# Branch A of a hybrid encoder layer: values, both tiles' transposes in three banks, then scores, in one step

## The chip, the cores and the metric

The kernel runs on one core of one Trainium2 chip. The metric is the device time of one execution in microseconds (us), the median of the runs; lower is better.

## The reference, cut to what matters

One encoder layer is computed for two inputs, a prompt of 256 rows and a sample of 1024 rows, each row 1024 wide, in float32. The layer has two attention branches beside each other, gates that merge them, an output projection, and an MLP with a squared ReLU. The change lies in branch A, a windowed attention with a sink: eight query heads over two key/value heads, 64 wide, each block of 128 rows looking at its own block of keys and the two next to it.

```python
s = jnp.einsum('bnqgrd,bnkgd->bngrqk', qb, kb).astype(jnp.float32) * (dh ** -0.5)
logits = jnp.where(valid[None, :, None, None], s + bias, NEG_INF)
m = jnp.maximum(jnp.max(logits, axis=-1), sink_r)
p = jnp.exp(logits - m[..., None])
denom = jnp.sum(p, axis=-1) + jnp.exp(sink_r - m)
o = jnp.einsum('bngrqk,bnkgd->bnqgrd', p.astype(vb.dtype), vb).astype(jnp.float32)
o = o / jnp.transpose(denom, (0, 1, 4, 2, 3))[..., None]
...
gates = jax.nn.sigmoid((z[..., o6:] + b_gate).astype(jnp.float32)).astype(x.dtype)
merged = gates[:, :, 0] * (o_a.reshape(b, S, A_Q) @ w_branch_a) + gates[:, :, 1] * (o_b @ w_branch_b)
x = x + merged @ w_out
```

## The kernel before, in words

The large products are split into a high and a low part and take three matmuls each; they fill most of the time. Branch A comes about a third of the way in, after the projections and branch B. From there on the instructions of each engine stand in the order in which the Python code writes them; there is no planner.

Branch A works on 40 tiles: four units (`u`, two query heads each) times ten tiles (`t`) of 128 query rows, eight of the sample and two of the prompt. A tile looks at two or three key blocks of 128, so it is 256 or 384 wide: tiles 0, 7, 8 and 9 of a unit are 256 wide, the others 384. For each tile there are four pieces of work:

- `scores` (lines 1116 to 1132): per head two matmuls on TensorE (PE) into a bank tagged `sc`, a custom VectorE (DVE) instruction that adds the bias and takes the row maximum (L1126), and one small DVE instruction for both heads that makes the negative maximum `nm_a` (L1130).
- `exponential` (L1136): per head one ScalarE (ACT) instruction in place on `s`, with the row sum.
- `transposes` (L1139): per head and key block one PE transposition of 128 x 128 (L1148), four or six in all, into two banks tagged `pt`. ACT empties the first bank (four transpositions, L274), DVE the second (two, L276; none for a tile 256 wide). They go to a buffer `pt` of six blocks, of which there are two.
- `values_of` (L1152): for a pair of tiles, the products of the transposed exponentials with the values (L1163) into the one bank tagged `pv`, a DVE copy to `o` (L1166) and a store that GpSimd (POOL) issues (L1167).

PSUM has eight banks: three tagged `mm`, two `sc`, two `pt`, one `pv`.

Between these pieces the loop (lines 1384 to 1419) draws portions of other work from two generators. `fill` is `logits`, the last five blocks of 128 columns of the gate logits: each `next(fill)` issues four matmuls 512 wide or eight 256 wide into an `mm` bank (L192). A block of 512 columns takes six portions, one of 256 columns three; each set of 128 gate columns has the blocks 512, 256, 512. Where a block is complete, the next call first writes ACT's copy to `gs` (L1188) and its store, and after the 256 block also the conversion of the next weights: `whi` on ACT (L231) and `wlo` on DVE (L235). `merges` is `merge`, which combines branch B's three groups: its later portions load `r` by SyncE's queue (L1284, L1287) and multiply and add on POOL (L1303, L1306).

The loop handles a pair of tiles per step, 20 steps and one more to empty the pipeline. A step at `j` computes scores for tiles `j` and `j + 1`, transposes tiles `j - 2` and `j - 1`, and multiplies out tiles `j - 4` and `j - 3`. Its order on PE is: scores of `j`, fill, values, fill, transposes of `j - 2`, scores of `j + 1`, fill, transposes of `j - 1`.

Of the kernel before, what the change touches and what calls it, by code (L numbers as in the profile page):

```python
# [97 lines left out]
def encoder_kernel(  # L98
# [37 lines left out]
    def bank(tag, name=None):  # L136
        return psum.tile([P, 512], F32, name=name or tag, tag=tag, bufs={"mm": 3, "sc": 2, "pt": 2, "pv": 1}[tag])
# [133 lines left out]
    def moved(eng, out, in_):  # L271

        if eng is nc.scalar:
            nc.scalar.activation(out, in_, AF.Copy)  # L274
        else:
            nc.vector.tensor_copy(out, in_)  # L276
# [825 lines left out]
    if True:  # L1102
# [3 lines left out]
        def a3(name, shape=(P, 2, 3 * P), n=3, dt=F32):  # L1106
            return att.tile(list(shape), dt, name=name, tag=name, bufs=n)
# [8 lines left out]
        def scores(u, t):  # L1116
            st, bias = units[u]
            lo, W, c0 = tiles[t]
            s = a3("s", n=3)
            m = small.tile([P, 2], F32, name="m", tag="m")  # L1120
            for h in range(2):
                ps = bank("sc")
                q = st["q"][h][:, P * t : P * t + P]
                nc.tensor.matmul(ps[:, :W], q, st["k"][1][:, P * lo : P * lo + W], start=True, stop=False)  # L1124
                nc.tensor.matmul(ps[:, :W], q, st["k"][0][:, P * lo : P * lo + W], start=False, stop=True)
                nc.vector.tensor_tensor_reduce(  # L1126
                    s[:, h, :W], ps[:, :W], bias[:, h, c0 : c0 + W], 1.0, -3.0e38,
                    op0=ALU.add, op1=ALU.max, accum_out=m[:, h : h + 1],
                )
            nc.vector.scalar_tensor_tensor(nm_a[:, 2 * u : 2 * u + 2, t], m, -1.0, nsink[:, 2 * u : 2 * u + 2],  # L1130
                                           op0=ALU.mult, op1=ALU.min)
            live[u, t] = s
# [5 lines left out]

        def transposes(u, t):  # L1139

            W = tiles[t][1]
            s = live[u, t]
            pt = a3("pt", (P, 6, P), 2)
            jobs = [(b, h) for b in range(W // P) for h in range(2)]
            for i, eng in ((0, nc.scalar), (4, nc.vector))[: 1 + (len(jobs) > 4)]:
                ps, e = bank("pt"), min(len(jobs), i + 4)
                for k, (b, h) in enumerate(jobs[i:e]):
                    nc.tensor.transpose(ps[:, P * k : P * k + P], s[:, h, P * b : P * b + P], ident)  # L1148
                moved(eng, pt[:, i:e, :], ps[:, : P * (e - i)].rearrange("p (i q) -> p i q", q=P))
            live[u, t] = pt  # L1150

        def values_of(u, t):  # L1152

            pv = bank("pv")
            for i in range(2):
                lo, W, _ = tiles[t + i]
                pt = live.pop((u, t + i))
                v, rest = units[u][0]["v"]
                for b in range(W // P):
                    k = lo + b  # L1160
                    src = v[:, k, HALVES[u // 2]] if k < 8 else rest[:, k - 8, HALVES[u // 2]]
                    for h in range(2):
                        nc.tensor.matmul(pv[HALVES[h], P * i : P * i + P], src, pt[:, 2 * b + h, :],  # L1163
                                         start=b == 0, stop=b == W // P - 1, skip_group_check=True)
# [159 lines left out]
    if True:  # L1324
# [57 lines left out]
        next(merges)  # L1382
        steps_of(fill, 2)
        for j in range(0, n + 2, 2):
            if j < n:
                scores(*order[j])
                next(fill)
                for h in range(2):
                    exponential(*order[j], h)
            if j > 2:  # L1390
                values_of(*order[j - 4])
                if j < n:
                    next(merges, None)
            next(fill)
            if j:
                transposes(*order[j - 2])
            if j == n:
                next(fill)
            if j < n:
                scores(*order[j + 1])  # L1400
                next(fill)
            if j:
                transposes(*order[j - 1])
                if j > 2:
                    next(merges, None)
            if j < n:
                for h in range(2):
                    exponential(*order[j + 1], h)
            if j == n - 4:
                high_b(0)  # L1410
                low_b(0)
            if j < n and order[j][1] == 0 and order[j][0] < 3:
                u = order[j][0] + 1
                units[u] = load_unit(u), load_bias(u, lambda name, shape: a3(name, shape, 2))
            if j in (n - 6, n - 4):
                fetch()
            if j == n - 2:
                load_o(0)
                load_o(1)
# [574 lines left out]
```

## Time and profile before

| | us |
|---|---|
| median of 3 runs | 1694.82 |
| lowest and highest | 1693.9 and 1695.1 |
| the profiled execution | 1694.27 |
| its span in the profile | 1692.5 |
| PE busy, share of the span | 1675.2, 99% |
| DVE busy | 953.4, 56% |
| ACT busy | 719.6, 43% |
| POOL busy | 513.1, 30% |
| branch A's loop, from the span's start | about 547 to 684 |

In the profile, a row of the timeline has the start and the duration in us, the engine, the source line, the operation, what it writes and reads, and a count where equal neighbours are merged; brackets hold the idle time of the engine ahead of it and what ended that. PEld is the load of a matmul's weights, which runs beside the matmul ahead of it. Matmuls overlap: the duration of one is longer than the distance to the next start, so distances between starts are what counts on PE.

### The profile page before, as it was taken

What the parts mean: (1) busy time and instruction counts of PE and PEld (TensorE: products, weight loads), DVE (VectorE), ACT (ScalarE), POOL (GpSimd) and SP (SyncE); (2) the same over time, 40 slices, a digit from 0 to 9 for tenths busy, and PEclk for the clock granted to TensorE, in tenths of its full rate; (3) what the DMA queues carried; (4) which work ended last, traced back from release to release, by engine and by line L of the source; (5) the groups of instructions that cost most, each with busy time, mean ns of one, the idle gap of its engine ahead of it and who ended that gap; (6) DMA issues with size and microseconds to landing.
All of it is one profiled execution on the core that took longest, in us unless ns stands there. A gap on an engine that the chain in (4) does not pass through costs nothing.

```text
span 1692.5 us, 24900 instructions
## 1 busy us (share of the span) xinstructions
PE 1675.2 (99%) x9268; PEld 1415.3 (84%) x9268; DVE 953.4 (56%) x1548; ACT 719.6 (43%) x1489; POOL 513.1 (30%) x404
## 2 busy tenths in 40 slices
PE   8999999999999999999999999999999999999998
PEld 7898888887778888888888888888888888888886
DVE  6732233445553565577278444545547867667575
ACT  6332323345563655654175333333334333333345
POOL 1312212212111463200100555546456332314150
PEclk9999999999999999999999999999999999999999
DMA  7426562566666793845121443443346845633333
GB/s 245 150 58 126 133 137 75 162 192 189 186 191 182 218 244 107 282 141 206 38 85 61 160 141 114 142 158 116 123 159 231 299 152 159 210 104 116 119 118 125
DMA packets 224409, 260.36 MB, mean 154 GB/s; under 512 B 29568, under 2 KB 154288, under 8 KB 224288
## 3 DMA queue, kind: packets, MB, share of 16 engines
q1 hardware_dynamic: 214976, 235.60, 44.1%
q0 software_dynamic: 7936, 20.54, 5.7%
q10 hardware_dynamic: 1376, 2.62, 0.4%
q8 instruction: 73, 1.20, 0.3%
q14 instruction: 48, 0.39, 0.1%
HBM read 173.03 MB, written 90.92 MB: 156 GB/s over the span
## 4 chain that ended last, share of the span: by engine, by line
PE 92%; DVE 3%; ACT 2%; DMA 1%; issue 1%; POOL 0%; SPq 0%; DVEq 0%; ACTq 0%
PE dn L349 20%; PE x L349 19%; PE mm L192 14%; PE z L349 9%; PE v L788 6%; PE mm L349 5%; PE y L349 5%; PE sc L349 3%; PE pv L349 3%; PE sc L538 1%; PE pv L1163 1%; PE pv L581 1%; PE pt L568 1%; PE pt L1148 1%; PE sc L1124 1%
## 5 line engine op out<-in xcount | busy, mean ns | idle before, releaser
L349 PE MATMUL dn<-dhi,ulo 128*128 128x512 f32 x448 | 174.6, 390 | 3.1 <-DVE ulo L186 3.1
L349 PE MATMUL dn<-dhi,uhi 128*128 128x512 f32 x448 | 174.3, 389 | 0.0
L349 PE MATMUL dn<-dlo,uhi 128*128 128x512 f32 x448 | 174.3, 389 | 0.0
L349 PE MATMUL x<-chi,wlo 128*128 128x512 f32 x424 | 167.4, 395 | 1.7 <-DVE wlo L316 1.6
L349 PE MATMUL x<-clo,whi 128*128 128x512 f32 x424 | 165.8, 391 | 0.1
L349 PE MATMUL x<-chi,whi 128*128 128x512 f32 x424 | 165.1, 389 | 0.0
L316 DVE TENSOR_TENSOR wlo<-ta,whi 128x1024 fp32r<-128x1024 f32 x30 | 55.8, 1859 | 180.4 <-ACT whi L314 180.4
L316 DVE TENSOR_TENSOR wlo<-raw,whi 128x1024 fp32r<-128x1024 f32 x60 | 91.3, 1522 | 101.1 <-ACT whi L314 101.1
L391 POOL TENSOR_TENSOR tb<-raw 128x512 f32<-128x512 f32 x25 | 32.6, 1304 | 364.5 <-DMA raw<-in_w_in_dram 145.2
L349 PEld LDWEIGHTS dn<-dhi,ulo 128*128 128x128 f32 x448 | 84.1, 188 | 21.6 <-DVE ulo L186 4.3
L186 DVE TENSOR_TENSOR ulo<-uraw,uhi 128x1024 fp32r<-128x1024 f32 x56 | 95.1, 1719 | 11.6 <-ACT uhi L185 11.6
L349 PEld LDWEIGHTS dn<-dhi,uhi 128*128 128x128 f32 x448 | 84.1, 188 | 17.5
L349 PEld LDWEIGHTS dn<-dlo,uhi 128*128 128x128 f32 x448 | 84.1, 188 | 17.4
L349 PEld LDWEIGHTS x<-chi,wlo 128*128 128x128 f32 x424 | 79.8, 188 | 20.0 <-issue 1.7
L349 PEld LDWEIGHTS x<-chi,whi 128*128 128x128 f32 x424 | 79.6, 188 | 17.0
L349 PEld LDWEIGHTS x<-clo,whi 128*128 128x128 f32 x424 | 79.8, 188 | 14.9 <-DVE clo L316 0.4
L1692 POOL TENSOR_TENSOR t<-raw,t 128x1024 f32<-128x1024 f32 x16 | 46.3, 2909 | 142.6 <-DMA raw<-in_w_down_dram 138.1
L1846 DVE TENSOR_TENSOR v<-v,dn 128x512 f32<-128x512 f32 x90 | 59.5, 681 | 39.8 <-PE dn L349 35.2
L558 ACT ACTIVATE s<-s,nm_b 128x128 f32<-128x128 f32 (+1 forms) x120 | 51.9, 434 | 54.4 <-DVE nm_b L550 54.4
L349 PE MATMUL dn<-dhi,up 128*128 128x512 f32 x224 | 73.5, 389 | 0.0
L1939 POOL TENSOR_TENSOR u<-u,u 128x640 f32<-128x640 f32 x16 | 25.6, 1597 | 156.5 <-ACT u L1864 156.5
L349 PE MATMUL z<-chi,wlo 128*128 128x512 f32 x184 | 72.1, 392 | 0.0
(325 smaller groups left out, 4651.4 us busy)
## 6 DMA issues: line engine op xcount, KB each, us to landing
scr_u<-u SPq DMA_DIRECT2D x112, 320.0 KB, 2.6
uraw<-scr_u SPq DMA_DIRECT2D x56, 512.0 KB, 4.5
raw<-in_w_in_dram SPq DMA_DIRECT2D x33, 512.0 KB, 5.9
raw<-in_w_up_dram SPq DMA_DIRECT2D x32, 512.0 KB, 5.3
raw<-in_w_down_dram SPq DMA_DIRECT2D x28, 512.0 KB, 6.6
sg<-scr_g SPq DMA_DIRECT2D x32, 256.0 KB, 6.2
uraw<-scr_u SPq DMA_DIRECT2D x28, 256.0 KB, 4.6
v<-scr_v SPq DMA_DIRECT2D x96, 64.0 KB, 2.8
```

Of the source, the lines that this page charges most:

```text
L186: nc.vector.tensor_tensor(lo, src, hi.bitcast(F32), op=ALU.subtract)
L192: nc.tensor.matmul(ps, a, b, start=i == 0, stop=i == len(seq) - 1)
L316: nc.vector.tensor_tensor(lo, src, hi.bitcast(F32), op=ALU.subtract)
L349: nc.tensor.matmul(ps, a, b, start=first and i == 0, stop=last and i == len(seq) - 1, skip_group_check=True)
L391: (nc.vector if vector else nc.gpsimd).tensor_tensor(o, x, y, op=ALU.subtract)
L538: nc.tensor.matmul(at(k, h)[p0 : p0 + nq, :], qk[rows, p0 : p0 + nq], qk[rows, P + P * a : P + P * a + W], start=True, stop=True, skip_gro ...
L558: nc.scalar.activation(s[:, h, :W], s[:, h, :W], AF.Exp, bias=nm[:, h : h + 1], accum_out=l[:, h : h + 1])
L568: nc.tensor.transpose(ps[:, P * a : P * a + P], s[:, h, P * k : P * k + P], ident)
L788: nc.tensor.matmul(ps[:, :n], a, b, start=k == 0 and j == 0, stop=k == KC - 1 and j == 2)
L1692: nc.gpsimd.tensor_tensor(o, a, b, op=ALU.subtract)
L1846: nc.vector.tensor_tensor(v, v, ps, op=ALU.add)
L1939: nc.gpsimd.tensor_tensor(u[S1], u21, u22, op=ALU.add)
```

## The change

The step's work is the same, in another order: values of the pair `j - 4`, transposes of both tiles `j - 2` and `j - 1`, scores of `j`, two portions of fill, exponentials of `j`, scores of `j + 1`, one portion of fill, exponentials of `j + 1`. The transposes of a pair (8, 10 or 12) go through two `pt` banks and, beyond eight, one `mm` bank, emptied by ACT, DVE and ACT, into a single buffer of twelve blocks in place of two of six.

```diff
         def transposes(u, t):
-            W = tiles[t][1]
-            s = live[u, t]
-            pt = a3("pt", (P, 6, P), 2)
-            jobs = [(b, h) for b in range(W // P) for h in range(2)]
-            for i, eng in ((0, nc.scalar), (4, nc.vector))[: 1 + (len(jobs) > 4)]:
-                ps, e = bank("pt"), min(len(jobs), i + 4)
-                for k, (b, h) in enumerate(jobs[i:e]):
-                    nc.tensor.transpose(ps[:, P * k : P * k + P], s[:, h, P * b : P * b + P], ident)
-                moved(eng, pt[:, i:e, :], ps[:, : P * (e - i)].rearrange("p (i q) -> p i q", q=P))
-            live[u, t] = pt
+            pt = a3("pt", (P, 12, P), 1)
+            jobs, at = [], []
+            for i in range(2):
+                at.append(len(jobs))
+                jobs += [(live[u, t + i], b, h) for b in range(tiles[t + i][1] // P) for h in range(2)]
+            for i, tag, eng in ((0, "pt", nc.scalar), (4, "pt", nc.vector), (8, "mm", nc.scalar)):
+                if i < len(jobs):
+                    ps, e = bank(tag, "pt"), min(len(jobs), i + 4)
+                    for k, (s, b, h) in enumerate(jobs[i:e]):
+                        nc.tensor.transpose(ps[:, P * k : P * k + P], s[:, h, P * b : P * b + P], ident)
+                    moved(eng, pt[:, i:e, :], ps[:, : P * (e - i)].rearrange("p (i q) -> p i q", q=P))
+            for i in range(2):
+                live[u, t + i] = pt, at[i]
...
         for j in range(0, n + 2, 2):
-            if j < n:
-                scores(*order[j])
-                next(fill)
-                for h in range(2):
-                    exponential(*order[j], h)
             if j > 2:
                 values_of(*order[j - 4])
                 if j < n:
                     next(merges, None)
-            next(fill)
             if j:
                 transposes(*order[j - 2])
-            if j == n:
-                next(fill)
             if j < n:
+                scores(*order[j])
+                steps_of(fill, 2)
+                for h in range(2):
+                    exponential(*order[j], h)
                 scores(*order[j + 1])
                 next(fill)
-            if j:
-                transposes(*order[j - 1])
                 if j > 2:
                     next(merges, None)
-            if j < n:
                 for h in range(2):
                     exponential(*order[j + 1], h)
+            else:
+                steps_of(fill, 2)
+                next(merges, None)
```

`values_of` reads each tile's blocks at its place `at` in the shared buffer.

More of the change, by code (lines that the diff above doesn't have):

```diff
@@ L1156, in values_of @@
                 lo, W, _ = tiles[t + i]
-                pt = live.pop((u, t + i))
+                pt, at = live.pop((u, t + i))
                 v, rest = units[u][0]["v"]
@@ L1162, in values_of @@
                     for h in range(2):
-                        nc.tensor.matmul(pv[HALVES[h], P * i : P * i + P], src, pt[:, 2 * b + h, :],
+                        nc.tensor.matmul(pv[HALVES[h], P * i : P * i + P], src, pt[:, at + 2 * b + h, :],
                                          start=b == 0, stop=b == W // P - 1, skip_group_check=True)
```

## The prediction

> **What bounds the kernel now.** I read the chain that ended last first, then the busy times of the stretch that the change edits, then who waited for whom there, and last the stretch instruction by instruction. The first two rows are the engines' shares of the chain, and the stretch of branch A (columns: PE, PEld, DVE, ACT and POOL busy with their counts, the granted clock, the DMA share, GB/s). The next three are all that PE and the weight loads waited for there.
>
> ```profile
> PE 92%; DVE 3%; ACT 2%; DMA 1%; issue 1%; POOL 0%; SPq 0%; DVEq 0%; ACTq 0%
> ...
> 545.00:684.20 139.20, 138.20 (x1097) 118.25 (x1096) 75.41 (x265) 81.43 (x221) 67.79 (x83) 1.00 0.70 192
> ...
> PE pt L1148 <- DVE pt L276: 0.5, 1, 0.5
> PE pv L1163 <- ACT pt L274: 0.4, 2, 0.3
> ```
>
> The reader is to see that PE sets the end, that it is busy for 138.20 of 139.20 us in this stretch at full clock, and that DVE (75.41) and ACT (81.43) have room. So the change can win only what lies between PE's matmuls, and it loses whatever PE newly waits for. PE takes its work in written order, so a transposition that waits holds everything behind it: the scores, the fill and the next step.
>
> **The change part by part.** I call S the scores of a tile, F one portion of the gate logits from `fill`, V the values of a pair, T a tile's transposes. A step goes from S F V F T S F T to V T T S F F S F. In both, a new block of the fill begins at the step's second F (two portions lie ahead of the loop, three in each step, and blocks take 6, 3 and 6). `merges` advances after V, ahead of that F, in both. So SP's order (loads of r, store of gs, load of raw), POOL's order and the order in which the shared w slots are taken are the same; I cost these queues at nothing. The single 12-wide `pt` replaces two 6-wide buffers that V reads just before T in either version: nothing.
>
> *Order on PE.* PE's starts around V:
>
> ```profile
> 633.01 0.39 PE L192 MATMUL mm<-hhi,whi 128*128 128x512 f32 x1
> 633.33 1.53 PE L1163 MATMUL pv<-pt,va 128*64 128x128 f32 x24
> 634.79 0.50 PE L192 MATMUL mm<-hhi,wlo 128*128 128x512 f32 x1
> 635.13 0.40 PE L192 MATMUL mm<-hlo,whi 128*128 128x512 f32 x1
> 635.36 0.39 PE L192 MATMUL mm<-hhi,whi 128*128 128x512 f32 x1
> 635.59 0.39 PE L192 MATMUL mm<-hhi,wlo 128*128 128x512 f32 x1
> 635.82 0.82 PE L1148 MATMUL pt<-ident,s 128*128 128x128 f32 x6
> 636.39 0.36 PE L1124 MATMUL sc<-kk,q 128*128 128x256 f32 x1
> ```
>
> One F matmul follows another after 0.23 us (635.13 to 635.36). The first behind V takes 0.34 (634.79 to 635.13), the last ahead of V 0.32. After the change V still follows F, but T follows V: the extra 0.11 goes. Six T take 0.57 to S (635.82 to 636.39), five of them 0.11 apart and the last only 0.02 or so; of two rounds now joined, one keeps a full 0.11, so about 0.08 is lost. Net 0.03 a step, over 20 steps -0.5 us. V directly ahead of T is not in this stretch: T may pay the same 0.11 as F did, or save as much again, so the bounds are +1.7 and -2.7 us; I take the row nearest to it, which is no surcharge.
>
> *Waits that go away.* One in the middle and two at the end:
>
> ```profile
> 629.73 0.66 PE L1148 MATMUL pt<-ident,s 128*128 128x128 f32 x4
> 630.90 0.44 PE L1148 MATMUL pt<-ident,s 128*128 128x128 f32 x2 [0.52 <-DVE pt L276]
> 631.38 0.44 PE L1124 MATMUL sc<-kk,q 128*128 128x384 f32 x1
> ...
> 677.75 0.60 PE L1148 MATMUL pt<-ident,s 128*128 128x128 f32 x4
> 678.63 1.31 PE L1163 MATMUL pv<-pt,va 128*64 128x128 f32 x20 [0.28 <-ACT pt L274]
> ...
> 682.80 0.66 PE L1163 MATMUL pv<-pt,vp 128*64 128x128 f32 x8
> 683.62 0.66 PE L1163 MATMUL pv<-pt,vp 128*64 128x128 f32 x8 [0.16 <-ACT pt L274]
> ```
>
> Six T took 1.65 us instead of 0.57: 1.1 lost, because the second round needed a bank that DVE had not emptied. Three banks used once a step remove that. At the end V stood right behind its own transposes: four T took 0.88 where 4 x 0.11 and a change of work of 0.1 make 0.54, so 0.34; eight V took 0.82 where 24 take 1.46 (0.49 for eight), so 0.33. After the change two F lie between (at the very end) or a whole step (before). Together -1.7 us.
>
> *The wait that comes.* Before, a tile's T came more than a whole round behind its S. Now the second tile's T follows its S with only F, V and the first tile's T between. The chain from S to the exponentials, where nothing was queued in its way:
>
> ```profile
> 616.77 0.42 PE L1124 MATMUL sc<-kk,q 128*128 128x384 f32 x1
> ...
> 618.57 1.09 PE L1163 MATMUL pv<-pt,vp 128*64 128x128 f32 x16
> 619.59 0.38 PE L192 MATMUL mm<-phi,wlo 128*128 128x256 f32 x1
> ...
> 617.51 0.56 DVE L1126 CUSTOM_DVE_ANT_0 s<-sc,bias 128x384 f32<-128x384 f32 x1 [0.69 <-PE sc L1125]
> ...
> 618.00 0.55 DVE L1126 CUSTOM_DVE_ANT_0 s<-sc,bias 128x384 f32<-128x384 f32 x1
> ...
> 618.59 0.16 DVE L1130 SCALAR_TENSOR_TENSOR nm_a<-m,nsink 128x2 f32<-128x2 f32 x1
> ...
> 618.85 0.61 ACT L1136 ACTIVATE s<-s,nm_a 128x384 f32<-128x384 f32 x1
> ...
> 619.46 0.60 ACT L1136 ACTIVATE s<-s,nm_a 128x384 f32<-128x384 f32 x1
> ```
>
> From S at 616.77 to the end of the second head's exponential at 620.06: 3.29 us. PE's cover is S and F, 1.80 (616.77 to 618.57), then V, 1.02 for 16 (618.57 to 619.59), 1.46 for 24 and 1.24 for the 20 between them, then the first tile's four or six T at 0.11. By pair of tiles: (0,1) 1.80 + 1.02 + 0.44 = 3.26; (2,3) 1.80 + 1.24 + 0.66 = 3.70; (4,5) 1.80 + 1.46 + 0.66 = 3.92. In (6,7) and (8,9) the second tile is 256 wide and its chain shorter. The second head's first T is one T later still. So undisturbed, three middle steps after (0,1) lose about 0.05 each, 0.15 in all, and the others have 0.4 to 0.6 us in hand. This small margin is the heart of the forecast.
>
> The first step has no V as cover:
>
> ```profile
> 550.03 0.33 PE L1124 MATMUL sc<-kk,q 128*128 128x384 f32 x1
> ...
> 551.66 0.34 PE L1124 MATMUL sc<-kk,q 128*128 128x384 f32 x1
> ...
> 552.47 0.60 ACT L1136 ACTIVATE s<-s,nm_a 128x384 f32<-128x384 f32 x1
> ```
>
> At 551.66, where the next S stood, T begins; the second tile's second head is wanted at 551.66 + 0.44 + 0.11 = 552.21 and ready at 553.07: +0.9 us, between 0.7 and 1.1.
>
> *Steps that prepare weights.* In four steps the second F also converts the next weights, on ACT and DVE:
>
> ```profile
> 593.46 0.36 ACT L1188 ACTIVATE gs<-mm 128x256 f32<-128x256 f32 x1
> 593.72 1.05 ACT L231 ACTIVATE whi<-raw 128x1024 fp32r<-128x1024 f32 x1
> ...
> 594.80 1.23 DVE L235 TENSOR_TENSOR wlo<-raw,whi 128x1024 fp32r<-128x1024 f32 x1 [1.05 <-ACT whi L231]
> 595.95 0.42 DVE L276 COPY pt<-pt 128x256 f32<-128x256 f32 x1
> ```
>
> Before, this lay behind V and only a copy of transposes was queued behind it. Now it lies between the two S: ACT's exponentials of the first tile and DVE's reductions of the second queue behind it. From gs to DVE's next instruction is 2.49 us. With S of the first tile at 0: S and F take 1.71 (1.80 less the 0.09 ahead of V), the last matmul drains, gs starts at 1.9, and the second S comes one F of 0.93 later, at 2.65; DVE is free at 4.4; the second tile's reductions, which would have begun at 2.65 + 0.74 = 3.4, begin there, and its exponentials end 2.55 later (617.51 to 620.06), at 6.95. T of its second head is wanted at 2.65 + 3.92 + 0.11 = 6.68. With the hand-over between engines that is 0.3 to 0.4 us, four times: +1.5 us, bounds 0 and 4 x 1.0.
>
> *What makes the chain longer.* DVE's small instruction between reductions and exponentials is the part that varies:
>
> ```profile
> 612.26 1.07 DVE L1130 SCALAR_TENSOR_TENSOR nm_a<-m,nsink 128x2 f32<-128x2 f32 x1
> ...
> 612.04 1.28 POOL L1303 TENSOR_TENSOR r<-r 128x512 f32<-128x512 f32 x1 [0.52 <-DMA r<-scr_c]
> ...
> L1130 DVE SCALAR_TENSOR_TENSOR nm_a<-m,nsink 128x2 f32<-128x2 f32 x40 | 13.7, 341 | 1.4
> L1306 POOL TENSOR_TENSOR merged<-merged,r 128x512 f32<-128x512 f32 x8 | 12.4, 1553 | 0.6
> L1303 POOL TENSOR_TENSOR r<-r 128x512 f32<-128x512 f32 x8 | 10.3, 1288 | 8.8 <-DMA r<-scr_c 8.7
> ```
>
> It takes 0.16 (618.59) or, when POOL multiplies, lasts until POOL has finished: 612.26 + 1.07 = 613.33, POOL 612.04 + 1.28 = 613.32. Forty take 13.7 us, so 7.3 above 40 x 0.16, half of it, 3.6, on second tiles. Before, nobody waited for that; now what exceeds the margin reaches PE. Bounds: 0 and, if POOL's instructions fall on each of the eight second tiles of its busy stretch, 8 x (1.3 - 0.4) = 7.2 us. I take +2.0, half of the 3.6 and a little for POOL's work now following V in fixed phase. The Trainium skill, "SBUF — State Buffer", section "Who interferes with whom", has a rule against this change: a DVE instruction with two SBUF inputs and a GpSimd instruction that reads SBUF exclude each other, and the later one blocks wholly. The two rows of 613.3 agree; by it the conversion at L235 would be held as well, and the sum would go towards the 7.2.
>
> **Sum.** -0.5 - 1.7 + 0.15 + 0.9 + 1.5 + 2.0 = +2.35 us. The profiled execution took 1694.27 us (span 1692.5 and 1.8 around it), so 1696.6; it lies 0.55 under the median of 1694.82, within the runs' spread. On the median the forecast is 1697.2, 0.14% more. A measurement of this kernel can tell about 0.2%, 3.4 us, from no change; so this is no change, leaning to slower.
>
> **The rivals.** *POOL in step with the second tile (slower).* POOL's two items a step, up to 2 x (1.29 + 1.55), could lie over the second tile's small instruction in every step of its stretch, and over the conversions. It decides once POOL holds DVE for over 0.4 us in most of these steps. For it: the 13.7 us; against it: POOL is paced by loads (8.7 us of idle), not by PE. 7.2 in place of 2.0: 1702.4.
>
> *The banks (slower).* The third bank of T comes from the fill's three. If a tag's banks are handed out in strict turn, then, four of five pairs taking one, the first block of each new 128 columns (four times) gets the very bank whose block has just ended, and PE waits for ACT to empty it: 0.39 for the last matmul (633.01) less 0.23, plus the copy:
>
> ```profile
> L1188 ACT ACTIVATE gs<-mm 128x512 f32<-128x512 f32 x8 | 4.6, 575 | 0.0
> ```
>
> 0.16 + 0.58 = 0.74, times four 3.0: 1700.2. Against it: if the longest free bank is taken, one is always empty. The Trainium skill, "Perfetto Trace Analysis", section "Optimization Strategy", reads equal gaps on the busy engine as a sign that the next tile found no buffer; before shows none here.
>
> *The margin holds (no change).* Chain and POOL cost nothing, only the first step does: -0.5 - 1.7 + 0.9 = -1.3, 1693.5.
>
> *Changes of work cost more than I see (faster).* V to T saves the further 2.2 and the margin holds: 1691.3. Against it: nothing in this stretch shows V directly ahead of T.
>
> **How the numbers follow.** Forecast 0.40, POOL in step 0.27, banks 0.13, margin holds 0.13, faster 0.07 (counting all of this last one beyond 0.2%). Slower by over 0.2%: 0.27 + 0.13 = 0.40. Within: 0.40 + 0.13 = 0.53. Faster: 0.07. The range leaves out the faster case and the upper part of the POOL case: 1693.2 to 1702.2.
>
> **What would show it.** In the profile after, PE's transposes (L1148 or its new line) should wait for ACT's exponentials, about 0.9 us at the first pair, 0.3 to 0.4 at four conversions, and now and then while POOL multiplies; waits for DVE's copy and at the last V should be gone. A wait of the fill's first matmul for gs would show the bank rival. I am wrong if those waits sum to under 1 or over 8 us, or if the step without waits is not within 0.1 us of the step before.

## The result, and the profile after

The changed kernel takes 1696.47 us in the median (1695.1 to 1700.58). The kernel before, run beside it, takes 1694.58. The ratio is 1.0013, with a 95% interval of 1.0007 to 1.0019: no change by the 0.2% that was set, on its slow side. The forecast was 1697.2 in a range of 1693.2 to 1702.2.

The first lines to read are the engines' shares of the chain that ended last, branch A's stretch (columns as before: PE, PEld, DVE, ACT and POOL busy with their counts, clock, DMA share, GB/s), and what PE and the weight loads waited for in it.

```profile
PE 89%; DVE 4%; ACT 2%; DMA 2%; issue 2%; SPq 1%; POOL 1%; DVEq 0%; ACTq 0%; POOLq 0%
...
545.00:686.20 141.20, 138.90 (x1099) 119.17 (x1098) 81.07 (x263) 80.03 (x217) 67.66 (x83) 1.00 0.69 193
...
PE pt L1150 <- ACT s L1136: 2.3, 8, 0.4
...
PEld pt L1150 <- ACT s L1136: 5.3, 16, 0.6
```

PE is still the bound, but it now has 2.3 us without work here where it had 1.0 in the shorter stretch of before, and all of it is one wait: transposes (now L1150) for exponentials (`s`, L1136). Both waits of before, for DVE's copy of transposes and of the values for ACT's, are gone. The weight loads, which run ahead of the matmuls, show the same wait as 5.3 us in 16 places. Before, their longest waits for data were 1.1 us in three places (values for exponentials), 0.9 in two (values for ACT's copy) and 0.8 in one (transposes for DVE's copy); the prediction's list has PE's waits alone.

How long the stage takes I read between two rows, the first scores and the first transposition of `wl`, which follows the last of the fill. First before, then after:

```profile
547.72 0.28 PE L1124 MATMUL sc<-kk,q 128*128 128x256 f32 x1
...
694.51 0.60 PE L1362 MATMUL pt<-ident,wl 128*128 128x128 f32 x4
```

```profile
547.86 0.28 PE L1124 MATMUL sc<-kk,q 128*128 128x256 f32 x1
...
696.21 0.60 PE L1365 MATMUL pt<-ident,wl 128*128 128x128 f32 x4
```

That is 146.79 us before and 148.35 after: the stage is 1.56 us longer. A little more is lost behind it, where the first products with the next weights wait for `wlo`:

```profile
710.34 0.50 PE L192 MATMUL mm<-ohi,wlo 128*128 128x512 f32 x1 [0.31 <-DVE wlo L235]
```

The profiled execution, at 1700.58 us, is the longest of the changed kernel's, because the clock dropped once far behind the change. The row of that stretch, in which 0.83 is the mean:

```profile
1330.00:1350.00 20.00, 17.52 (x64) 13.54 (x64) 17.89 (x17) 3.30 (x4) 5.93 (x2) 0.83 1.05 369
```

In the kernel before the same stretch has 1.00. From 1335.51 to 1341.22 the matmuls start 0.43 apart instead of 0.23; just ahead of that PE had started 0.8 late, waiting for DVE's `ulo`. By the positions of the matmuls on either side all of it cost 3.9 us. The change edits nothing there.

**The waits, one by one.** Transpositions that wait for nothing start 0.11 us apart, but for the second one behind values, which starts 0.17 after the first in every step. What they start later than 0.11 is counted here. The first step:

```profile
551.81 0.60 PE L1150 MATMUL pt<-ident,s 128*128 128x128 f32 x4
...
552.76 0.33 PE L1150 MATMUL pt<-ident,s 128*128 128x128 f32 x1 [0.35 <-ACT s L1136]
...
553.36 0.77 PE L1150 MATMUL pt<-ident,s 128*128 128x128 f32 x5 [0.27 <-ACT s L1136]
```

The fifth transposition was due at 551.81 + 0.44 = 552.25 and starts at 552.76. The sixth was due at 552.87 and starts at 553.36. That makes 0.51 + 0.49 = 1.0 us. The brackets show less than this, since the idle time begins only when the last matmul has drained.

A step that converts weights, at the place where POOL also multiplies:

```profile
597.00 0.34 PE L1124 MATMUL sc<-kk,q 128*128 128x384 f32 x1
...
597.64 1.23 DVE L235 TENSOR_TENSOR wlo<-raw,whi 128x1024 fp32r<-128x1024 f32 x1 [1.43 <-ACT whi L231]
...
598.78 0.55 DVE L1126 CUSTOM_DVE_ANT_0 s<-sc,bias 128x384 f32<-128x384 f32 x1
...
599.31 1.27 POOL L1306 TENSOR_TENSOR merged<-r 128x512 f32<-128x512 f32 x1 [4.88 <-DMA r<-scr_c]
...
599.86 0.75 DVE L1130 SCALAR_TENSOR_TENSOR nm_a<-m,nsink 128x2 f32<-128x2 f32 x1
...
600.20 0.88 PE L1150 MATMUL pt<-ident,s 128*128 128x128 f32 x6
...
601.31 0.60 ACT L1136 ACTIVATE s<-s,nm_a 128x384 f32<-128x384 f32 x1
...
601.46 0.33 PE L1150 MATMUL pt<-ident,s 128*128 128x128 f32 x1 [0.38 <-ACT s L1136]
...
602.05 0.77 PE L1150 MATMUL pt<-ident,s 128*128 128x128 f32 x5 [0.27 <-ACT s L1136]
```

The scores at 597.00 are reduced only at 598.78, behind `wlo`, which itself waited for `whi`. The small instruction then takes 0.75 instead of 0.16, and ends with POOL's multiplication (599.86 + 0.75 = 600.61, POOL 599.31 + 1.27 = 600.58). PE loses 601.46 - (600.20 + 0.66) = 0.60 and 602.05 - 601.57 = 0.48, together 1.08 us. The other three conversions lose less. These are the rows of the first of them, and behind them the one step without a conversion that lost much, with POOL in it:

```profile
566.66 1.00 PE L1150 MATMUL pt<-ident,s 128*128 128x128 f32 x7
567.93 0.76 PE L1150 MATMUL pt<-ident,s 128*128 128x128 f32 x5 [0.27 <-ACT s L1136]
...
652.73 0.80 POOL L1309 TENSOR_TENSOR merged<-merged,r 128x256 f32<-128x256 f32 x1
653.00 0.55 DVE L1130 SCALAR_TENSOR_TENSOR nm_a<-m,nsink 128x2 f32<-128x2 f32 x1
654.02 0.77 PE L1150 MATMUL pt<-ident,s 128*128 128x128 f32 x5
655.01 0.76 PE L1150 MATMUL pt<-ident,s 128*128 128x128 f32 x5 [0.22 <-ACT s L1136]
```

Seven transpositions at 0.11 are 0.77. So the first conversion loses 567.93 - 567.43 = 0.50, the third and fourth in the same way 0.61 (at 635.71) and 0.56 (at 669.69), and the step with POOL 655.01 - 654.57 = 0.44. With the first step and the 1.08 that makes 4.2 us in six steps. Two small things cancel in it: five of the six figures contain the 0.06 of the second transposition behind values, which is no wait, and all six leave out about 0.06 by which the transposition behind the last wait starts late. No other step lost over 0.1 us by waiting there, and nowhere did the fill wait for `gs`.

### The profile page after: what moved, and what is told of

Its sections match the earlier page's. It is cut to its first block, busy times and chain, and to the rows that moved or that the text cites. A ratio compares the mean times of both kernels' runs of the same rounds, so it can differ in the third digit from the quotient of the medians.

```text
span 1698.8 us, 24884 instructions
## 1 busy us (share of the span) xinstructions
PE 1678.9 (99%) x9268; PEld 1417.6 (83%) x9268; DVE 957.2 (56%) x1544; ACT 718.1 (42%) x1485; POOL 513.0 (30%) x404
## 4 chain that ended last, share of the span: by engine, by line
PE 89%; DVE 4%; ACT 2%; DMA 2%; issue 2%; SPq 1%; POOL 1%; DVEq 0%; ACTq 0%; POOLq 0%
PE dn L349 20%; PE x L349 18%; PE mm L192 13%; PE z L349 9%; PE v L788 5%; PE mm L349 5%; PE y L349 5%; PE sc L349 2%; PE pv L349 2%; PE pt L1150 1%; PE sc L538 1%; PE pv L1166 1%; PE pv L581 1%; PE pt L568 1%; PE sc L1124 1%
## 5 line engine op out<-in xcount | busy, mean ns | idle before, releaser
L185 ACT ACTIVATE dhi<-raw 128x1024 fp32r<-128x1024 f32 x32 | 33.5, 1058 | 93.1 <-PE dn L349 85.3
```

What stands on the lines that cost most here:

```text
L185: nc.scalar.activation(hi, src, AF.Copy)
```

## The experiments

My theory: what the change costs is that the second tile's exponentials come too late for its transposes, in the first step, at the four conversions, and where POOL holds DVE's small instruction. Against it stood the order of work on PE, the banks, and POOL as the main cost. All runs were made beside the kernel before, and ratios are to it. Differences of a few tenths of a us between medians lie near what these runs can tell. So each verdict rests on the places where PE waits, and on the length of the stage, from first scores to first `wl` transposition (148.35 us in the changed kernel, 146.79 before). All edits are to the changed kernel.

**Another phase of the fill, first try.** Four portions ahead of the loop, so that the conversions fall at another place in the step.

```diff
-        steps_of(fill, 2)
+        steps_of(fill, 4)
```

> The changed kernel, with two more portions of fill ahead of the loop, so that a new block of the fill, and with it the conversion of weights, falls on the third portion of a step, behind the second tile's reductions. Theory (the second tile's chain is late because the conversion stands in it): the waits of the transpositions at the four conversions (0.45, 1.0, 0.5 and 0.5 us in the trace after) go, the one of the first step (1.0) stays; 2.0 to 2.5 us under the changed kernel, about 1694.2. Rival (POOL's multiplications make the chain late, wherever the conversion is): these waits stay in the stretch in which POOL multiplies; at most 1 us under the changed kernel, 1695.5 to 1696.5. Rival (the order on PE costs more than its waits): no wait left at the conversions, but the time stays at 1696.5.

Measured: 1703.46, ratio 1.0052 (1.0039 to 1.0066), 7.0 us above the changed kernel. The stage takes 148.75 us although two portions, 1.86 us of work, have moved ahead of it. The profiled execution (1701.17) is 4.4 us behind the changed kernel's at the end of the `wl` transpositions: 2.3 in the stage, counting the work moved, 0.6 ahead of it and 1.6 behind it. At three of the four conversions the waits inside the transposes did go. At the third, 1.4 us are left (633.47 and 634.07), and others came between 610 and 626. On SP's queue a store of `gs` now stood ahead of the next unit's loads:

```profile
574.47 0.39 SPq L222 DMA_DIRECT2D raw<-in_w_in_dram  x1
587.47 0.32 SPq L1192 DMA_DIRECT2D scr_g<-gs  x1
587.84 0.45 SPq L427 DMA_DIRECT2D kk<-scr_ka  x1
...
609.39 1.26 POOL L1306 TENSOR_TENSOR merged<-r 128x512 f32<-128x512 f32 x1 [13.04 <-DMA r<-scr_b]
```

For 13 us the queue starts nothing, until `gs` is written, and POOL's multiplication comes at 609.39, ten us later than the 599.31 above. POOL's work is then crowded, and holds DVE and PE. This run changed two things, so it settles neither.

**Another phase, second try.** One portion ahead of the loop, so that one portion of 0.93 us more lies within the stage.

```diff
-        steps_of(fill, 2)
+        steps_of(fill, 1)
```

> The changed kernel, with one portion of fill fewer ahead of the loop, so that new blocks fall on the third portion of the same steps as in the changed kernel (in e1 they fell one step earlier, and the store of gs stood in front of the next unit's loads on SyncE's queue). Theory: the four conversions' waits (2.5 us) go, nothing else moves, and POOL's work keeps its time: 1.5 to 2.5 us under the changed kernel, 1694.0 to 1695.0. Rival (a conversion behind the second scores is as bad, by what it does to the next step): at or above the changed kernel, 1696.5 or more.

Measured: 1694.82, ratio 1.0004 (0.9995 to 1.0013). The stage takes 146.25 us, and without the added portion 145.32: 3.0 less than in the changed kernel. What PE waited for, and the transposes of the step that lost 1.08:

```profile
PE pt L1150 <- ACT s L1136: 0.6, 2, 0.3
...
599.02 1.53 PE L1150 MATMUL pt<-ident,s 128*128 128x128 f32 x12
```

Twelve transpositions run in one piece. The four conversions' waits are gone. The list has only the first step's two (0.6); by the starts one more is left, 0.24 us at 618.96. Where the conversions stand in the step decides whether they cost anything. At 599 POOL's hold is gone too, but by its timing and not by more room in the chain. Its multiplication started together with `wlo`, at 597.70, and was itself held:

```profile
597.70 2.36 POOL L1306 TENSOR_TENSOR merged<-r 128x512 f32<-128x512 f32 x1 [4.44 <-DMA r<-scr_c]
```

So the 1.08 of that step is no clean test of the conversion; the other three, 1.67 us together, are.

**The first step alone.** Only at the first transposes, two portions of fill go ahead of them instead of behind the scores.

```diff
+            if j == 2:
+                steps_of(fill, 2)
             if j:
                 transposes(*order[j - 2])
             if j < n:
                 scores(*order[j])
-                steps_of(fill, 2)
+                steps_of(fill, 0 if j == 2 else 2)
```

> The changed kernel, but in the first step with transposes the two portions of fill stand ahead of them. Theory: only the first step's wait goes (1.0 us), all others stay as they are: 1695.5. Rival (that wait is covered by work that is only moved, so that the later steps wait longer): 1696.5.

```profile
554.11 1.25 PE L1150 MATMUL pt<-ident,s 128*128 128x128 f32 x10
...
556.40 0.44 PE L1124 MATMUL sc<-kk,q 128*128 128x384 f32 x1 [0.34 <-DVE m L1126]
```

The first ten transpositions run in one piece, so that wait is gone. In its place the second scores, now directly behind the first, wait once for a `sc` bank and lose 0.5. Median 1695.97, ratio 1.0008 (0.9999 to 1.0016); the stage takes 147.31 us, 1.04 less. 1.0 is won and 0.5 given back. Another 0.5 came from chance: at the second conversion POOL's multiplication started behind `wlo`, was held by it (2.09 us) and missed the small instruction, and that step lost 0.51 instead of 1.08.

**POOL's hold.** The small instruction with two SBUF tensors is replaced by two with one tensor and a scalar per row.

```diff
-            nc.vector.scalar_tensor_tensor(nm_a[:, 2 * u : 2 * u + 2, t], m, -1.0, nsink[:, 2 * u : 2 * u + 2],
-                                           op0=ALU.mult, op1=ALU.min)
+            for h in range(2):
+                c = slice(2 * u + h, 2 * u + h + 1)
+                nc.vector.tensor_scalar(nm_a[:, c, t], m[:, h : h + 1], -1.0, nsink[:, c],
+                                        op0=ALU.mult, op1=ALU.min)
```

> The changed kernel, with the small DVE instruction that makes nm_a replaced by two that take one tensor and one scalar per row each. Theory (it is the second SBUF tensor that makes DVE wait for POOL): no such instruction takes over 0.2 us while POOL multiplies; the extra 0.6 us at the second conversion and the 0.4 us at the first pair of the fourth unit go, for 0.1 us a tile on the chain: 0 to 1 us under the changed kernel, 1695.5 to 1696.5, and the waits at conversions are equal, about 0.5 each. Rival (DVE is slow there for another reason): the long ones stay, 1696.5 to 1698.

Median 1695.06, ratio 1.0003 (0.9995 to 1.0012); the stage takes 146.99 us, 1.36 less. The group of the small instruction, first in the changed kernel, then here, with the conversion that POOL had made longer:

```profile
L1130 DVE SCALAR_TENSOR_TENSOR nm_a<-m,nsink 128x2 f32<-128x2 f32 x40 | 13.0, 326 | 1.4
```

```profile
L1132 DVE TENSOR_SCALAR nm_a<-m,nsink 128x1 f32<-128x1 f32 x80 | 13.3, 208 | 0.0
...
599.62 0.33 DVE L1132 TENSOR_SCALAR nm_a<-m,nsink 128x1 f32<-128x1 f32 x2
...
600.08 0.98 PE L1152 MATMUL pt<-ident,s 128*128 128x128 f32 x7
601.28 0.77 PE L1152 MATMUL pt<-ident,s 128*128 128x128 f32 x5 [0.22 <-ACT s L1138]
```

Two take 0.33 at a place where one took 0.75, and that step now loses 601.28 - 600.85 = 0.43 instead of 1.08. It becomes like the other conversions, and the 0.44 of the step at 655 is gone. So POOL's hold is about 0.65 + 0.44 = 1.1 us of what PE lost, and the conversions are the larger part. The Trainium skill, "SBUF — State Buffer", section "Who interferes with whom", says that a DVE instruction with at most one SBUF input, outside its two-port modes, does not contend with GpSimd. With this the trace agrees: 80 of them average 208 ns and none takes over 211, while the 40 with two inputs average 326 and one alone takes 160.

**Two banks.** The third group of transpositions takes a `pt` bank instead of an `mm` bank.

```diff
-            for i, tag, eng in ((0, "pt", nc.scalar), (4, "pt", nc.vector), (8, "mm", nc.scalar)):
+            for i, tag, eng in ((0, "pt", nc.scalar), (4, "pt", nc.vector), (8, "pt", nc.scalar)):
```

> The changed kernel, with the third group of transposes in a pt bank instead of an mm bank, two banks in all. Theory (the third bank is what lets both tiles' transposes follow each other): PE waits for ACT to empty the first bank, about 0.44 + 0.25 + 0.65 us after the first transposes against 0.87 when the third group is due, 0.4 to 0.5 us in each of 16 steps; 7 us over the changed kernel, about 1703, and the waits for late exponentials shrink in these steps. Rival (the transposes wait for exponentials anyway): 1697.

```profile
PE pt L1150 <- ACT pt L274: 3.7, 14, 0.3
```

Median 1704.95, ratio 1.0062 (1.0048 to 1.0076); the stage takes 6.8 us more. A new wait, for ACT to empty the first bank, appears in each step that has more than eight transpositions (16 of 20). In 14 it is long enough to leave PE empty and costs 0.37 to 0.48 us, in the other two 0.1. So the third bank is needed for transposes in one piece, and it took nothing from the fill: the changed kernel never waits for `gs`.

**The order of before, with joined transposes.** Scores, fill, values, fill, both tiles' transposes, scores, fill.

```diff
         for j in range(0, n + 2, 2):
+            if j < n:
+                scores(*order[j])
+                next(fill)
+                ...
             if j > 2:
                 values_of(*order[j - 4])
                 ...
+            next(fill)
             if j:
                 transposes(*order[j - 2])
             if j < n:
-                scores(*order[j])
-                steps_of(fill, 2)
-                ...
                 scores(*order[j + 1])
                 next(fill)
...
             else:
-                steps_of(fill, 2)
+                next(fill)
```

> The order of before with one thing changed: both tiles' transposes together, through three banks into one buffer, where the first tile's stood; values and first scores keep their places. Theory (the gain of three banks is the waits of before, 1.7 us; the loss is only that transposes come soon after the second scores): all those waits go and no new one comes; order on PE within 0.1 us a step of before; 1.0 to 2.0 us under before, about 1693. Rival (the third bank or the joined round costs by itself): 1695 to 1697.

My theory fell here. The transposes wait no longer, but the kernel gains nothing over before: 1695.08, ratio 1.0002 (0.9993 to 1.001), and a stage of 148.16 us, hardly under the 148.35. The second scores took over the wait, at two of the four conversions. The first line is a conversion without that wait, the others are one with it:

```profile
561.83 1.23 DVE L235 TENSOR_TENSOR wlo<-raw,whi 128x1024 fp32r<-128x1024 f32 x1 [1.03 <-ACT whi L231]
...
595.07 1.29 POOL L1306 TENSOR_TENSOR merged<-r 128x512 f32<-128x512 f32 x1
...
595.24 2.21 DVE L235 TENSOR_TENSOR wlo<-raw,whi 128x1024 fp32r<-128x1024 f32 x1 [1.03 <-ACT whi L231]
597.37 0.68 DVE L276 COPY pt<-pt 128x512 f32<-128x512 f32 x1
...
598.58 0.44 PE L1124 MATMUL sc<-kk,q 128*128 128x384 f32 x1 [0.76 <-DVE m L1126]
```

POOL held the conversion itself this time (2.21 us against 1.23; POOL starts 0.17 earlier), and so it did at the other one with the wait (2.17). DVE then had a copy of four transpositions before it reduced the first scores. Only then was a `sc` bank empty for the second. The longest matmul gaps there were 1.16 and 1.53 us. At the conversions of 1.23, at 561.83 and 664.55, the same row of a conversion, a copy and two reductions cost PE about 0.2 us (from values to values 7.12 and 7.18 in place of 6.93 in before). So two `sc` banks nearly cover that row, and it is POOL's hold of about 1 us that they do not cover.

**Values and transposes in the middle.** Scores, two portions of fill, values, transposes, scores, fill: V and T stay together as in the change, but the first scores stand ahead of them.

```diff
         for j in range(0, n + 2, 2):
+            if j < n:
+                scores(*order[j])
+                steps_of(fill, 2)
+                for h in range(2):
+                    exponential(*order[j], h)
             if j > 2:
                 ...
             if j:
                 transposes(*order[j - 2])
             if j < n:
-                scores(*order[j])
-                steps_of(fill, 2)
-                for h in range(2):
-                    exponential(*order[j], h)
                 scores(*order[j + 1])
```

> Scores of the first tile, two portions of fill, values, both tiles' transposes, scores of the second tile, one portion. Theory: as much order gained as in the changed kernel (0.5 us), the waits of before gone (1.7), and no new ones, since a scores, three portions and the values stand between the second scores and its transposes: about 2.2 us under before, 1692.4. Rival (values directly ahead of transposes cost on PE): not under before, 1694.6.

```profile
583.60 0.69 DVE L276 COPY pt<-pt 128x512 f32<-128x512 f32 x1
...
584.81 0.44 PE L1124 MATMUL sc<-kk,q 128*128 128x384 f32 x1 [0.63 <-DVE m L1126]
```

No transposition waits. One wait is left. DVE's row of work is again too long for the `sc` banks, this time without POOL: nine small instructions of `merge` (581.91 to 583.69) stand ahead of DVE's copy. Median 1693.62, ratio 0.9996 (0.9988 to 1.0005); the stage takes 145.06 us, 3.3 less than in the changed kernel and 1.7 less than before.

A variant drew both portions of `merges` behind the second scores (its edit is shown against the one above):

```diff
             if j > 2:
                 values_of(*order[j - 4])
-                if j < n:
-                    next(merges, None)
...
                 if j > 2:
-                    next(merges, None)
+                    steps_of(merges, 2)
```

> As e6 (scores, two portions, values, both transposes, scores, one portion), but the first of the two portions of merges stands with the second, behind the second scores. In e6 one wait was left, 0.9 us, where DVE's part of merges stood ahead of the second tile's reductions. Theory: it goes, and the gain over before in the stretch grows from 1.4 to 2.2 us: about 1692.3. Rival (POOL's work then comes later and in one piece, and the loads of r with it): not under e6, 1693.5 or more.

That wait went, and a shorter one (0.48 in its bracket) came at a conversion, at 630.77. There `wlo` was hardly held (1.27 us), but DVE had two copies behind it, of values and of transposes. The stage takes 144.72 us. Median 1693.37, ratio 1.0003 (0.9994 to 1.0011): the medians of the two can't be told apart.

**Fill between values and transposes.** One of the two portions behind the first scores is moved ahead of the transposes.

```diff
+            if j and j < n:
+                next(fill)
             if j:
                 transposes(*order[j - 2])
             if j < n:
                 scores(*order[j])
-                steps_of(fill, 2)
+                steps_of(fill, 1 if j else 2)
```

> One of the two fill portions between the scores moves to a place between the values and the transposes; SP's and POOL's orders stay. Theory (the transposes wait for the second tile's exponentials, 0.47 us over the margin at a conversion): a portion of 0.93 us more of cover ends the waits inside the transposes in every step; what of the first step is left is under 0.1 us. Against that stands one change of kind of work more in each step (values to fill and fill to transposes for values to transposes), about 0.08 us a step, 1.6 in all: the stage ends 4.9 less 1.6 = 3.3 us earlier than in the changed kernel, about 1.7 before the kernel before; median 1693 to 1694.5. Rival (the cost is in the order or the banks, not in the exponentials): the waits stay and the median is at or over 1696.5.

```profile
597.84 1.53 PE L1166 MATMUL pv<-pt,va 128*64 128x128 f32 x24
599.30 0.50 PE L192 MATMUL mm<-hhi,whi 128*128 128x512 f32 x1
599.64 0.40 PE L192 MATMUL mm<-hhi,wlo 128*128 128x512 f32 x1
...
600.34 1.47 PE L1150 MATMUL pt<-ident,s 128*128 128x128 f32 x12
```

In this stage PE waits nowhere: the list of its waits is empty. Median 1693.07, ratio 0.9991 (0.9982 to 1.0), 3.4 us below the changed kernel; the stage takes 145.11 us, 3.2 less. The price is in the same rows: the fill's second matmul behind the values starts 0.34 after the first instead of 0.23. Against that, the transpositions no longer follow values: twelve take 1.47, and 1.53 behind values in the second phase's run. So the price is 0.11 less 0.06, 0.05 a step, 1 us over 19 steps. Then 4.2 us of late starts must have gone, which is the sum of the six steps above. The expectation had 4.9 and 1.6 for the two; both were too large by 0.6 to 0.7, and only the difference came out. This confirms the theory by adding cover, where the second phase did it by moving the work that delayed the chain.

**Two remedies together.** The late phase and the one-tensor form; and the one-tensor form with values and transposes in the middle.

```diff
-        steps_of(fill, 2)
+        steps_of(fill, 1)
...
-            nc.vector.scalar_tensor_tensor(...)
+            for h in range(2):
+                nc.vector.tensor_scalar(...)
```

> The late phase of the fill (one portion ahead of the loop instead of two) and the small instruction with one SBUF tensor instead of two, together. Theory: the conversions' waits go with the first (2.6 us of the stage in its own run), POOL's hold on the small instruction with the second (1.3 in its own run); both shared the waits at the conversions, so less than the sum of 3.9: the stage ends 3 to 3.5 us earlier than in the changed kernel, 1.5 to 2 before the kernel before, with only the first step's 1.0 us of waits inside the transposes; median 1693 to 1694. Rival (the two edits took away the same waits): no more than the better of them, the stage 1.0 before the kernel before, median 1694.5 or more.

Median 1693.05, ratio 0.9992 (0.9983 to 1.0001). The stage takes 145.81 us, and 144.88 without the added portion: 3.5 less than in the changed kernel, 1.9 less than before, and 0.4 less than with the late phase alone. Only the first step's waits are left inside the transposes. One more wait stands in its list, 1.17 us at 547.18 for ACT's `z` (L989), but it lies ahead of the stage, where the fill begins behind other work on an `mm` bank. In the late phase alone this is 0.23. It is a part of what moves the stage's start from one execution to the next, and the reason why the stage is read from its first scores. So the two remedies together save less than the sum of what they save alone (3.0 and 1.36), and more than either, as the theory had it.

The second combination is the edit of "values and transposes in the middle" and that of "POOL's hold", both unchanged.

> Values and transposes between the second fill portion and the second scores, and the small instruction with one SBUF tensor. Theory: with this order no transpose waited in its own run, so POOL's hold reached nobody and the one-input form wins nothing more there: the stage 1.5 to 2.0 us before the kernel before, median 1693 to 1694, and the one wait of the second scores for DVE's merge work stays. Rival (POOL's hold still reaches PE by the second scores' bank): 0.5 to 1 us less than that, median under 1693.

```profile
PE sc L1124 <- DVE m L1126: 1.1, 2, 0.6
```

Both expectations missed: 1695.06, ratio 1.0002 (0.9993 to 1.0011), and a stage of 146.04 us, 1.0 more than with the order alone and 0.75 less than before; the profiled execution took 1693.89. The wait at `merge`'s work stays, and a second one comes at a conversion, where `wlo` took 2.28 us beside POOL. Whether the longer small work (0.33 instead of 0.16 where nothing holds it) brought that about, or POOL's timing in this execution, one run cannot say.

## Why the prediction was right

Its direction and its mechanism held: waits taken away, and new ones of the transposes for exponentials at the three kinds of places it named. That the sum came within 0.8 us is in part luck: POOL's hold was put 0.9 too high and the conversions 0.6 too low, and the order came out by two errors that cancel. Neither sign of being wrong that it named appeared: the new waits sum to 4.2 us, between 1 and 8, and the step without waits is within 0.05 us of the step before. Term by term, in us:

| step of the sum | forecast | measured |
|---|---|---|
| order on PE | -0.5 | -0.7 to -0.9 |
| waits of before that go | -1.7 | -1.7 |
| margin of the steps after the first pair | +0.15 | under 0.1 |
| first step | +0.9 | +1.0 |
| four conversions | +1.5 | +2.1 |
| POOL's hold | +2.0 | +1.1 |
| sum | +2.35 | +1.6 to +1.8; the stage is 1.56 longer |

*Order.* Five steps without a wait over 0.1, from values to values, in the second phase's run, and the same five of before:

```profile
637.73 1.53 PE L1166 MATMUL pv<-pt,va 128*64 128x128 f32 x24
...
670.72 1.53 PE L1166 MATMUL pv<-pt,va 128*64 128x128 f32 x24
```

```profile
640.03 1.53 PE L1163 MATMUL pv<-pt,va 128*64 128x128 f32 x24
...
673.20 1.53 PE L1163 MATMUL pv<-pt,va 128*64 128x128 f32 x24
```

32.99 against 33.17 us, so -0.04 a step and -0.7 in 20. The same five with values and transposes in the middle, a step with the same changes of work, take 32.94 (640.65 to 673.59): -0.05 and -0.9. The lines of the values changed number, the work did not. The size is right, but both of its steps were wrong. V directly ahead of T is not free: the second T pays 0.06 (0.17 in place of 0.11), where F paid 0.11. And joining two rounds loses nothing: the last T of a round saves 0.08, but the S behind it pays it back. In the changed kernel the second score matmul starts 0.26 after the first behind T (553.88 to 554.14) and 0.18 behind F (556.53 to 556.71). So a step gains 0.05 by V alone, where the forecast had 0.11 less 0.08.

*Conversions.* The mechanism was right and the size was low: 0.50, 0.61, 0.56 and, without POOL, 0.43, in place of 0.3 to 0.4. DVE is free 1.78 behind the second scores (597.00 to 598.78), where the forecast had 1.75, and from there to the end of the exponentials it takes 601.31 + 0.60 - 598.78 = 3.13, 2.54 without the 0.59 of holding, where the forecast had 2.55. What was short is the hand-over to PE: the exponentials end at 601.91, the transposition starts at 602.05. These 0.14 on top of the forecast's 6.95 - 6.68 = 0.27 make 0.41, about what the step lost without POOL (0.43). Why the other three lost 0.1 to 0.2 more is not shown.

*POOL.* This term was too large. The forecast put half of the holding on second tiles. Of the 13.0 - 40 x 0.16 = 6.6 us in the changed kernel 2.1 fell on second tiles, and only two holds met one without room in hand (599.86 and 653.00). Of the other four, three met tiles 256 wide, and one a tile 384 wide with 0.4 in hand, which it used 0.2 of. The rest fell on first tiles, whose transposes come later. So the rival in which POOL keeps step with the second tile did not happen: the small instruction's 13.0 us are less than the 13.7 of before. The point named from which it decides, 0.4 us, was hardly tested: the two holds that cost something met a conversion and the pair (0,1), for which the forecast had no margin, so the 0.39 beyond 0.16 at 653 cost its full size, 0.44. The trace agrees with the rule on two SBUF inputs that the prediction takes from the Trainium skill ("SBUF — State Buffer", section "Who interferes with whom"). What it would have added through the conversion did not happen in the changed kernel, whose `wlo` took 1.23 each time. It did in three other runs: the first phase (2.59), the joined transposes (2.21 and 2.17) and the last combination (2.28).

*The other rivals.* Banks: no wait for `gs`, and with two `pt` banks the wait that comes is for another copy. The Trainium skill, "Perfetto Trace Analysis", section "Optimization Strategy", says that equal gaps on the busy engine can mean a shortage of buffers. With two banks the trace agrees; in the changed kernel three gaps of 0.50 to 0.61 look just as equal and come from a dependency, as the moved phase shows. Margin holds and changes of work that save more: the order's measured -0.7 to -0.9 and the 4.2 us of waits exclude both.

*What was not foreseen.* The forecast treated the conversion as a delay of the second tile's chain alone. Where T's cover is made longer, DVE's row of work at a conversion can delay the `sc` banks instead. It did so where POOL held the conversion (twice with the joined transposes, once in the last combination) or where two copies stood behind it (630.77). This does not touch the sum of the change, but it is why the joined transposes in the old order gained nothing: the two held conversions cost 1.2 and 1.5 us there.

The medians moved by 1.89 us, the stage by 1.56. The profiled execution loses 0.5 more by the end of the `wl` transpositions, one wait of which was shown at 710.34; why that conversion came later was not tried.

## What to carry to other kernels

Before joining two rounds of work on the busy engine, take the longest chain that now has to fit between its producer and its consumer, and add to it what else the helper engines must do at that point in some steps only: here the weights' conversion in four steps of twenty cost 2.1 us, while most of the other steps had room. Where such a chain is short by half a microsecond, put other work of the busy engine into the gap or shift the rare work by a portion, and look afterwards at who waits next: three orders took the waits from the transposes, and two of them found the scores waiting for the same engine. The best version here puts one portion of fill between values and transposes; it has no wait left in the stage, and is 0.09% ahead of the kernel before, with an interval that ends at 1.0, so no run shows it clearly faster.

## What the runs showed of the hardware

A small DVE instruction with two SBUF tensors is held while POOL multiplies, and so is a large one: 0.16 became 0.75 and 0.55, and `wlo` went from 1.23 to 2.21 and 2.28. Which of the two waits went by who started first: POOL at 595.07 held `wlo` of 595.24 (2.21 us), and `wlo` of 597.74, in the run on the first step, held POOL's multiplication of 598.01 (2.09 in place of 1.27). Rewritten with one tensor and a scalar per row, the small one was not held at all (211 ns at most in 80).

Some changes of kind of work on PE show only at the second matmul, in starts. Behind values, the second fill matmul starts after 0.34 instead of 0.23 and the second transposition after 0.17 instead of 0.11; behind transpositions, the second score matmul after 0.26 instead of 0.18, but there the first comes 0.08 earlier (0.03 behind the last transposition).

A weight load that waits tells more than the matmul behind it: with matmuls in flight, PE's own list showed 2.3 us where the starts of the transpositions had moved by over 4. The list of the weight loads showed 5.3, more than was lost.

In one profiled execution the matmuls ran at about half their pace for 6 us (0.43 between starts in place of 0.23; the mean granted clock over 20 us was 0.83) and came back by themselves. The rows behind and ahead of it were at 1.00. It began behind a start that was 0.8 late; nothing in the trace shows that this was the cause.
